# A hybrid attention layer in 4,804 matmuls: four edits to the order of weight splits, squares and loads

## The chip, the cores and the metric

The kernel runs on one core of a Trainium2 chip. The metric is the device time of one execution in microseconds (us); before the change it is 887.37 us, the median of three runs (884.22, 887.37, 887.9).

## What is computed

One decoder layer on 512 tokens of width 1024, in float32. Two token mixers run on the same normalised rows: gated linear attention (GLA, 4 heads, chunked) and multi-head latent attention (MLA, 8 heads, causal softmax). Each output is projected back, the two are merged by sigmoid gates, and projected once more. Then follows a squared-ReLU MLP of width 4096. Layer norms stand in front of the mixers and behind both sub-layers.

```python
h = layer_norm(x, ln_in_g, ln_in_b)
q_g, k_g, v_g, r_g, a_lr, q_lat, kv_lat, gate_logits = split(h @ w_in)
o_gla = rms_norm(gla_chunked(q_g * HK**-0.5, k_g, v_g, log_a), gla_norm_g)
y_gla = (o_gla * silu(r_g)) @ w_o_gla
q = rms_norm(q_lat, q_a_norm_g) @ w_q_b               # nope part, rope part
kv = rms_norm(kv_lat[..., :256], kv_a_norm_g) @ w_kv_b # k_nope, v
o_mla = causal_softmax_attention(q, k_nope, k_rope, v)  # blocks of 128 queries
y_mla = o_mla @ w_o_mla
mix = (g_gla * y_gla + g_mla * y_mla) @ w_out
h = layer_norm(ALPHA * h + mix, ln1_g, ln1_b)
h = layer_norm(ALPHA * h + square(relu(h @ w_ff1)) @ w_ff2, ln2_g, ln2_b)
```

## The kernel before

Every matmul keeps float32 precision with three products in a faster format: an operand is split into a rounded part `hi` and the rest `lo`, and the kernel adds hi x hi, hi x lo and lo x hi. So each weight tile passes through one fixed path. SP issues the load of a 512 KB raw tile (`wraw`, L175). ACT copies it to the rounded format (`whi` or `xh`, L190). DVE subtracts that from the raw tile (`wlo` or `xl`, L191). Then PE multiplies: L246 to L248 in `gemm_fm`, which puts features on the partitions, and L280 to L282 in `gemm_tm`, which puts tokens there.

All weight tiles stand in one list, `stream`, in the order in which the products use them. `pump(i)` is called as a product reaches tile i: it issues loads two tiles ahead and the splits one tile ahead (`DMA_AHEAD, SPLIT_AHEAD = 2, 1`). Tiles marked `res` are resident: they are split into buffers of their own. Everything else runs in generators that `tick` steps between the products of a weight tile. A scheduler then reorders the instructions of each engine, within the dependences and within the orders that `tc.issue_after` fixes; `issue_after` orders two instructions of the same engine and makes no engine wait for another. Entries of `st["gates"]` are such orders for the next split.

The places that the change touches, in order of time:

- The first layer norm. `ln_transpose` transposes each of eight 128-column blocks of the normalised rows on PE (L449), and evicts it: ACT writes the hi part `h` (L452) and, for some blocks, the temporary `lnt` (L454); DVE writes the other `lnt` (L456) and the lo part (L457). The products of the latent projections (`PL["lat", i]`, `gemm_tm`) take these blocks as they come. The two first tiles of q's weights follow in `stream`, and their splits are issued while these products run.
- GLA's output, `gla_out`, once for each of four heads. Four row blocks i of 128 tokens are computed (L891 to L893); blocks 0 and 1 share one PSUM tile, and so do 2 and 3. ACT squares each block with a sum (`osq`, L895); POOL raises the sums to the power -1/2, and DVE scales the blocks. Two lanes of generators share PE here: one for the heads' scores, one for these outputs.
- MLA. For each head and each block of queries PE computes the scores (L1006 to L1010), for block 0 with a reduce on DVE (L1003); DVE adds the mask and takes the maximum (`mx`, L1013), ACT the exponential (`Pm`, L1016), DVE the division (L1018). PE transposes the probabilities (L1030), and `split` writes them as `PT` (hi on ACT at L111, lo on DVE at L112). The products with v follow (L1049 to L1051). Beside the heads run the output products of GLA (`yg`) and MLA (`ym`), two halves of 512 columns each, with four weight tiles in a half. Scores, transposes and products with v share one ring of PSUM buffers, `px`.
- The middle layer norm (LN1) and the MLP's start. The first `w_ff1` products begin on half of the tokens, while the second half is still being normalised. Their first tiles are resident (`xh`, `xl`). At `ci == 0` of the loop over MLP slices, `win_load(0)` has POOL issue eight loads of `w_ff2`, 512 KB each (`wq`, L1425); `win_sums` on DVE (L1433) reads them later. POOL also computes the powers for the norm's rows (L433, two for each half of the tokens); DVE's L439 normalises the rows.

Of the kernel before, what the change touches and what calls it, by code (L numbers as in the profile page):

```python
# [10 lines left out]
F32 = mybir.dt.float32  # L11
# [4 lines left out]
AF = mybir.ActivationFunctionType  # L16
ALU = mybir.AluOpType
AX = mybir.AxisListType

P = 128  # L20
T = 512
# [6 lines left out]
HV = 256  # L28
# [24 lines left out]
def tile_hybrid_block(ctx: ExitStack, tc: tile.TileContext, I, out, dbg=None):  # L53
    nc = tc.nc
# [22 lines left out]
    def B(shape, dt=F32, n="b"):  # L77
        return pb.tile(shape, dt, tag="B", name=nm(n))

    def S(shape, dt=F32, n="s"):  # L80
        return sm.tile(shape, dt, tag=n, name=nm(n))
# [11 lines left out]
    def f(ap):  # L93
        return ap.bitcast(F32)

    act = nc.scalar.activation
    vtt = nc.vector.tensor_tensor
# [10 lines left out]

    def split(src, hi, lo, scale=None):
        if scale is None:  # L110
            act(hi, src, AF.Copy)  # L111
            return vtt(lo, src, f(hi), op=ALU.subtract)  # L112
        else:
            act(hi, src, AF.Copy, scale=scale)  # L114
            return stt(lo, src, scale, f(hi), op0=ALU.mult, op1=ALU.subtract)
# [22 lines left out]
    stream = []  # L138
    st = {"dma": 0, "spl": 0, "gates": ()}
# [38 lines left out]
    def pump(i):  # L178
        fetch(i + 1 + DMA_AHEAD)
        while st["spl"] < min(len(stream), i + 2 + SPLIT_AHEAD):  # L180
            e = stream[st["spl"]]
            if st["spl"] > i + e.get("ahead", SPLIT_AHEAD) and not e["res"]:
                break
            nk, n = e["nk"], e["n"]
            hi, lo = [A([P, nk, T * 2 // nk], F32R, w) for w in HOME["a" if e["res"] else e.get("home", "w")]]
            raw = e["src"]() if "src" in e else e.pop("raw")
            with ExitStack() as gates:
                for g in st["gates"]:
                    gates.enter_context(tc.issue_after(g.ins))
                st["ins"] = act(hi[:, :nk, :n], raw[:, :nk, :n], AF.Copy)  # L190
                st["lo"] = vtt(lo[:, :nk, :n], raw[:, :nk, :n], f(hi[:, :nk, :n]), op=ALU.subtract)  # L191
            st["gates"] = ()
            e["w"] = (hi, lo)
            if "post" in e:
                e["post"](raw)
            if "post2" in e:
                later[st["spl"] + 2] = lambda p=e["post2"], r=raw: p(r)
            later.pop(st["spl"], lambda: None)()
            st["spl"] += 1
# [11 lines left out]
    def spawn(g):  # L211
        active.append(g)
        return g
# [13 lines left out]
    def finish(*gs):  # L227
        while any(g in active for g in gs):
            for g in list(active):
                if g in gs:  # L230
                    step(g)
# [68 lines left out]
    half = LAT // 2  # L300
    PL = {}
# [92 lines left out]
    for mb in range(2):  # L394
        PL["ym", mb] = plan("w_o_mla", mb * T, T)

    def plan_zip(key, specs):
        pls = [{"idx": [], "nk": 8, "per": 2} for _ in specs]
        for k0 in range(0, 8, 2):
            for j, (name, c0, kb, res) in enumerate(specs):  # L400
                pls[j]["idx"] += plan(name, c0, T, kb + k0, kb + k0 + 2, res=res)["idx"]
        PL[key] = pls
# [39 lines left out]
    def ln_transpose(rows, g, b, outs, hf, alt=False, n="h0"):  # L442
        tk = slice(hf * 256, (hf + 1) * 256)
        for k in range(NK):
            if len(outs) <= k:
                outs.append(A([P, 2, T], F32R, n) if n == "h0" else (B([P, T], F32R, n), B([P, T], F32R, n)))
            p = MM() if alt and k in (4, 5) else PX()
            for i in range(2):
                nc.tensor.transpose(p[:, i * P:(i + 1) * P], rows[2 * hf + i][:, k * P:(k + 1) * P], ident)  # L449
            tmp = B([P, 256], F32, "lnt")  # L450
            hi, lo = part(outs[k], 0, tk), part(outs[k], 1, tk)
            ha = act(hi, p[:, :256], AF.Identity, scale=g[:, k:k + 1], bias=b[:, k:k + 1])  # L452
            if (alt or n == "h1") and k % 2:
                act(tmp, p[:, :256], AF.Identity, scale=g[:, k:k + 1], bias=b[:, k:k + 1])  # L454
            else:
                vts(tmp, p[:, :256], g[:, k:k + 1], b[:, k:k + 1], op0=ALU.mult, op1=ALU.add)  # L456
            hd = vtt(lo, tmp, f(hi), op=ALU.subtract)  # L457
            if n == "h1":
                st["ln"] = (ha, hd)
            yield hd  # L460

    mvin = consts.tile([P, NT, 2], F32, name="mvin")
# [73 lines left out]
    def ev_lat(i):  # L536
        def e(a, j, ps):
            if lat[a] is None:
                lat[a] = A([P, LAT], F32, "lat")
            if (a + i) % 2 == 0:  # L540
                nc.vector.tensor_copy(lat[a][:, i * half:(i + 1) * half], ps[:, :half])
            else:
                act(lat[a][:, i * half:(i + 1) * half], ps[:, :half], AF.Copy)
        return e
# [149 lines left out]
    def r_prep():  # L694
        for (fn, *args), wait in zip(((r_load, "t2"), (r_acc, "t2", "11"), (r_load, "t1"), (r_acc, "t2", "22"), (r_load, "t3"),
                                      (r_acc, "t1", "11"), (r_acc, "t3", "22")), RY):
            fn(*args)
            for _ in range(wait):
                yield
# [171 lines left out]
    def gla_out(h):  # L871
        while SS[h] is None or Vh[h] is None or rgn[h] < NT:
            yield
        sd, s128, s256 = SS[h]

        def blk(j, i, w):
            if i == j:
                return sd[:, w, i, :]
            if j // 2 == i // 2:
                return s128[:, w, j // 2, :]  # L880
            return s256[:, w, j, (i - 2) * P:(i - 1) * P]

        vh, vl = Vh[h]
        ss = S([P, NT], F32, "gss")
        ps = []
        for i in range(NT):
            if i % 2 == 0:
                ps.append(PX())
            o = ps[i // 2][:, (i % 2) * HV:(i % 2 + 1) * HV]
            for j in range(i + 1):  # L890
                mm(o, blk(j, i, 0), vh[:, j, :], start=j == 0, stop=False)  # L891
                mm(o, blk(j, i, 0), vl[:, j, :], start=False, stop=False)
                mm(o, blk(j, i, 1), vh[:, j, :], start=False, stop=j == i)  # L893
            sq = B([P, HV], F32, "osq")
            act(sq, o, AF.Square, accum_out=ss[:, i:i + 1])  # L895
            if i >= 1:
                yield
        vts(ss, ss, 4.0 / HV, 4.0 * RMS_EPS, op0=ALU.mult, op1=ALU.add)
        rs = S([P, NT], F32, "grs")
        gtt(rs, ss, mhalf[:, :NT], op=ALU.pow)  # L900
        yield
        og = [B([P, 2, HV], F32, "og") for _ in range(2)]
        for i in range(NT):
            o = ps[i // 2][:, (i % 2) * HV:(i % 2 + 1) * HV]
            stt(og[i // 2][:, i % 2, :], o, rs[:, i:i + 1], Rg[h][:, i, :], op0=ALU.mult, op1=ALU.mult)
        yield
        for kk in range(2):
            k = 2 * h + kk
            p = PX()
            for tt in range(NT):  # L910
                nc.tensor.transpose(p[:, tt * P:(tt + 1) * P], og[tt // 2][:, tt % 2, kk * P:(kk + 1) * P], ident)
            yield
            o = A([P, 2, T], F32R, "ogT")
            split(p, o[:, 0, :], o[:, 1, :], scale=glg[:, k:k + 1])
            ogT[k] = o
# [70 lines left out]
    def mla_head(h, hl, qn, kn, vt):  # L986
# [39 lines left out]
        for b, (pl, pt) in enumerate(zip(plan_t, PT)):  # L1026
            n = len(pl) * P
            p = PX()
            for cc, j, i in pl:
                nc.tensor.transpose(p[:, cc * P:(cc + 1) * P], Ps[i][:, j * P:(j + 1) * P], ident)  # L1030
            split(p[:, :n], pt[:, 0, :], pt[:, 1, :])
            if b != 1:
                yield
        PT0, PT1, PT2 = PT
# [68 lines left out]
    for hf in range(2):  # L1103
        if hf == 1:
            finish(t_ln1)
            t_prep = spawn(prep())
            t_rp = spawn(r_prep())
        for i in range(2):
            gemm_tm([PL["lat", i]], hT, half, ev_lat(i), tts=(2 * hf, 2 * hf + 1))
    t_lat = spawn(latents())  # L1110
    t_he = spawn(h_early())
    gemm_fm(PL["q"], hT, T, ev_q)
# [306 lines left out]
    def win_load(ci):  # L1419
        w2 = I["w_ff2"].rearrange("(k p) n -> p k n", p=P)  # L1420
        for op, i, j in (("12", 0, 1), ("11", 0, 0), ("22", 1, 1), ("21", 1, 0)):
            for hf in range(2):
                t = A([P, 2, T], F32, "wq")
                k0 = 8 * ci + 4 * hf + i
                nc.gpsimd.dma_start(t, w2[:, k0:k0 + 3:2, j * T:(j + 1) * T])  # L1425
                WQ[("f2", ci), (op, hf)] = t
# [106 lines left out]
    for ci in range(FC):  # L1533
# [1 line left out]
        hid = []  # L1535
        win = ci < FC - 1
        if ci == 0:
            win_load(0)

        def ev_h(a, ps):  # L1540
            r = B([P, T], F32, "relu")
# [127 lines left out]
```

## Time and profile before

| | before |
|---|---|
| median of 3 runs | 887.37 us (884.22 to 887.9) |
| profiled execution | 886.19 us, of which the span is 884.3 us |
| PE busy | 863.6 us (98% of the span) |
| DVE, ACT, POOL busy | 639.8, 469.5, 197.7 us |
| mean granted clock of PE | 0.996 |
| bytes moved | 134.60 MB, 152 GB/s on average |

PE is TensorE, PEld its weight loads, DVE VectorE, ACT ScalarE, POOL GpSimd and SP SyncE. A timeline row gives the start in us from the span's start, the duration, the engine, the source line, the operation, what it writes and reads with shapes, how often, and in brackets the engine's idle time before it with what ended it. PEclk is the share of the full clock that the throttle granted to PE. A row with "x4" stands for four like instructions, and its duration is that of all four.

### The profile page before, as it was taken

How to read it: one execution, taken by the hardware profiler on the slowest of the kernel's cores; microseconds unless marked ns; L12 is line 12 of the kernel's file. 1: busy time of each engine (PE TensorE's matmuls, PEld its weight loads, DVE VectorE, ACT ScalarE, POOL GpSimd, SP SyncE). 2: the span in 40 equal slices, each digit the busy share in tenths (PEclk: the TensorE clock that was granted, in tenths of full speed). 3: DMA queues.
4: the chain of work that ended last, by engine and by line, in shares of the span. 5: the costliest groups of instructions: out<-in, count | busy, mean ns of one | idle time of the engine just before them, and what ended most of it. 6: DMA issues, size and time to landing. Idle time of an engine off the chain costs nothing.

```text
span 884.3 us, 13010 instructions
## 1 busy us (share of the span) xinstructions
PE 863.6 (98%) x4804; PEld 754.6 (85%) x4804; DVE 639.8 (72%) x1042; ACT 469.5 (53%) x823; POOL 197.7 (22%) x225
## 2 busy tenths in 40 slices
PE   6999999999999999999999999999999999999996
PEld 5988888889999978888888888988888888889985
DVE  7849969968665646757776796987557646788865
ACT  5546756646475634435554414566357546656820
POOL 1223637944201030300000013004400520141001
PEclk9999999999999999999999999999999999999999
DMA  7994936694738454322216527006941990399312
GB/s 242 281 228 136 321 117 151 221 247 147 216 71 223 126 148 103 102 66 72 78 41 249 187 83 275 1 1 168 292 111 30 263 252 28 83 233 232 119 62 82
DMA packets 95504, 134.60 MB, mean 152 GB/s; under 512 B 12960, under 2 KB 58400, under 8 KB 95440
## 3 DMA queue, kind: packets, MB, share of 16 engines
q1 hardware_dynamic: 73840, 92.36, 33.1%
q0 software_dynamic: 19392, 37.76, 19.9%
q10 hardware_dynamic: 2208, 3.66, 1.2%
q8 instruction: 38, 0.62, 0.3%
q14 instruction: 26, 0.21, 0.1%
HBM read 110.15 MB, written 8.91 MB: 135 GB/s over the span
## 4 chain that ended last, share of the span: by engine, by line
PE 93%; DVE 3%; DMA 2%; ACT 1%; issue 1%; POOL 0%; POOLq 0%; SPq 0%; DVEq 0%; ACTq 0%
PE mm L246 11%; PE mm L247 11%; PE mm L248 11%; PE mm L280 4%; PE mm L282 4%; PE mm L281 4%; PE mm L1194 4%; PE mm L1196 4%; PE mm L1195 4%; PE px L1482 2%; PE px L1481 2%; PE px L1480 2%; PE px L848 2%; PE mm L1482 2%; PE mm L1481 2%; PE mm L1480 2%
## 5 line engine op out<-in xcount | busy, mean ns | idle before, releaser
L191 DVE TENSOR_TENSOR wlo<-wraw,whi 128x1024 fp32r<-128x1024 f32 (+1 forms) x90 | 100.4, 1116 | 87.0 <-ACT whi L190 83.5
L190 ACT ACTIVATE whi<-wraw 128x1024 fp32r<-128x1024 f32 (+1 forms) x90 | 85.4, 949 | 86.4 <-PE mm L247 43.4
L246 PE MATMUL mm<-h,whi 128*128 128x512 f32 x224 | 87.3, 390 | 0.0
L247 PE MATMUL mm<-h,whi 128*128 128x512 f32 x224 | 87.2, 389 | 0.0
L248 PE MATMUL mm<-h,wlo 128*128 128x512 f32 x224 | 83.0, 390 | 0.0
L1499 POOL DMA_DIRECT2D res<-ev x42 | 36.8, 994 | 178.9 <-ACT ev L1497 143.4
L191 DVE TENSOR_TENSOR wlo<-wq,whi 128x1024 fp32r<-128x1024 f32 x44 | 54.5, 1239 | 30.1 <-ACT whi L190 30.1
L190 ACT ACTIVATE whi<-wq 128x1024 fp32r<-128x1024 f32 x44 | 46.5, 1057 | 26.1 <-PE mm L1195 16.1
L1195 PE MATMUL mm<-sh,whi 128*128 128x256 f32 x176 | 49.9, 283 | 0.0
L1196 PE MATMUL mm<-sh,wlo 128*128 128x256 f32 x176 | 49.9, 283 | 0.0
L1194 PE MATMUL mm<-sh,whi 128*128 128x256 f32 x176 | 49.9, 283 | 0.0
L248 PEld LDWEIGHTS mm<-h,wlo 128*128 128x128 f32 x224 | 42.0, 188 | 9.0 <-DVE wlo L191 0.4
L247 PEld LDWEIGHTS mm<-h,whi 128*128 128x128 f32 x224 | 42.1, 188 | 8.7
L246 PEld LDWEIGHTS mm<-h,whi 128*128 128x128 f32 x224 | 42.1, 188 | 8.7
L190 ACT ACTIVATE xh<-wraw 128x1024 fp32r<-128x1024 f32 (+1 forms) x28 | 27.3, 984 | 28.8 <-PE mm L282 14.5
L433 POOL TENSOR_TENSOR mv<-mv,mhalf 128x1 f32<-128x1 f32 x4 | 4.1, 1031 | 164.7 <-DVE mv L432 164.7
L191 DVE TENSOR_TENSOR xl<-wraw,xh 128x1024 fp32r<-128x1024 f32 (+1 forms) x28 | 31.3, 1129 | 10.6 <-ACT xh L190 10.6
L792 ACT ACTIVATE E<-rp 128x256 f32<-128x256 f32 x64 | 26.0, 418 | 22.5 <-POOL rp L787 15.6
L1542 ACT ACTIVATE relu<-mm 128x512 f32<-128x512 f32 x24 | 14.1, 596 | 41.5 <-PE mm L248 41.5
L786 POOL TENSOR_TENSOR rp<-rp 128x256 f32<-128x256 f32 x32 | 30.0, 937 | 25.4 <-ACT E L792 16.7
L787 POOL TENSOR_TENSOR rp<-rp 128x256 f32<-128x256 f32 x32 | 33.7, 1053 | 7.4 <-ACT q L817 3.8
L962 POOL DMA_DIRECT2D QS<-q x32 | 16.1, 509 | 85.3 <-ACT q L114 82.1
(477 smaller groups left out, 2816.6 us busy)
## 6 DMA issues: line engine op xcount, KB each, us to landing
wraw<-in_w_ff_dram SPq DMA_DIRECT2D x36, 512.0 KB, 5.0
wraw<-in_w_in_dram SPq DMA_DIRECT2D x30, 512.0 KB, 4.8
wq<-in_w_ff_dram POOLq DMA_DIRECT2D x26, 512.0 KB, 9.8
res<-ev POOLq DMA_DIRECT2D x42, 256.0 KB, 10.1
wq<-in_w_in_dram SPq DMA_DIRECT2D x20, 512.0 KB, 6.7
wq<-in_w_in_dram POOLq DMA_DIRECT2D x18, 512.0 KB, 10.5
hsd<-hs SPq DMA_DIRECT2D x16, 256.0 KB, 4.9
xr<-hsd SPq DMA_DIRECT2D x16, 256.0 KB, 4.1
```

The costliest lines, as they stand in the source:

```text
L190: st["ins"] = act(hi[:, :nk, :n], raw[:, :nk, :n], AF.Copy)
L191: st["lo"] = vtt(lo[:, :nk, :n], raw[:, :nk, :n], f(hi[:, :nk, :n]), op=ALU.subtract)
L246: mm(o, hi[:, c], xh, start=first, stop=False)
L247: mm(o, hi[:, c], xl, start=False, stop=False)
L248: mm(o, lo[:, c], xh, start=False, stop=last)
L280: mm(o, xh, hi[:, :n], start=opens, stop=False, skip_group_check=share)
L281: mm(o, xh, lo[:, :n], start=False, stop=False, skip_group_check=share)
L282: mm(o, xl, hi[:, :n], start=False, stop=last, skip_group_check=share)
L1194: mm(oa, hi[:, k, c], xh, start=opens and k == 0 and a == 0, stop=False, skip_group_check=True)
L1195: mm(oa, hi[:, k, c], xl, start=False, stop=False, skip_group_check=True)
L1196: mm(oa, lo[:, k, c], xh, start=False, stop=k == 3, skip_group_check=True)
L1499: nc.gpsimd.dma_start(res[tt + t][:, j * T:(j + 1) * T], e, accum_op=ALU.add)
```

## The change

Four edits; all computed values stay the same.

1. `ln_transpose` keeps the two instructions that evict block 5 of the first half of the tokens. `lat_guard`, called at the end of the products of the second latent tile, puts the next split (the second q tile's) behind those two, each in its engine's order.
2. In `gla_out` the square of block 0 is issued behind the products of block 1, together with block 1's own square, in each head. The sums and the number of instructions stay as they are.
3. The weight tiles of `yg` half 1 and of both halves of `ym` are split one 512-column half at a time, hi then lo (12 instructions more on ACT, 12 more on DVE). The second tile of `ym` half 0 is split behind the last pair of instructions that wrote transposed probabilities, `st["pt"]`.
4. At `ci == 0` POOL copies one column of the lo part of the third `w_ff1` tile to a 128x1 tile, `tok`, and the first loads of `w_ff2` are placed behind that copy in POOL's order. The copy needs DVE's subtraction of that tile, so here POOL does wait for another engine.

Order and number of all other instructions: PE has the same 4,804 matmuls. On PE, ACT and DVE the order of the two builds differs up to the end of the LN1 stretch and is the same from there on. SP's order differs by one exchange of two neighbouring loads.

```diff
@@ -108,7 +108,7 @@
 
     def split(src, hi, lo, scale=None):
         if scale is None:
-            act(hi, src, AF.Copy)
+            st["hi"] = act(hi, src, AF.Copy)
             return vtt(lo, src, f(hi), op=ALU.subtract)
         else:
             act(hi, src, AF.Copy, scale=scale)
@@ -185,10 +185,11 @@
             hi, lo = [A([P, nk, T * 2 // nk], F32R, w) for w in HOME["a" if e["res"] else e.get("home", "w")]]
             raw = e["src"]() if "src" in e else e.pop("raw")
             with ExitStack() as gates:
-                for g in st["gates"]:
+                for g in st["gates"] or (st.get("pt", ()) if e.get("late") else ()):
                     gates.enter_context(tc.issue_after(g.ins))
-                st["ins"] = act(hi[:, :nk, :n], raw[:, :nk, :n], AF.Copy)
-                st["lo"] = vtt(lo[:, :nk, :n], raw[:, :nk, :n], f(hi[:, :nk, :n]), op=ALU.subtract)
+                for k in [slice(i, i + 1) for i in range(nk)] if e.get("fine") else [slice(0, nk)]:
+                    st["ins"] = act(hi[:, k, :n], raw[:, k, :n], AF.Copy)
+                    st["lo"] = vtt(lo[:, k, :n], raw[:, k, :n], f(hi[:, k, :n]), op=ALU.subtract)
             st["gates"] = ()
             e["w"] = (hi, lo)
             if "post" in e:
@@ -394,6 +395,11 @@
     for mb in range(2):
         PL["ym", mb] = plan("w_o_mla", mb * T, T)
 
+    for key in (("yg", 1), ("ym", 0), ("ym", 1)):
+        for i in PL[key]["idx"]:
+            stream[i]["fine"] = True
+    stream[PL["ym", 0]["idx"][1]]["late"] = True
+
     def plan_zip(key, specs):
         pls = [{"idx": [], "nk": 8, "per": 2} for _ in specs]
         for k0 in range(0, 8, 2):
@@ -457,6 +463,8 @@
             hd = vtt(lo, tmp, f(hi), op=ALU.subtract)
             if n == "h1":
                 st["ln"] = (ha, hd)
+            elif hf and k == 5:
+                st["h0"] = (ha, hd)
             yield hd
 
     mvin = consts.tile([P, NT, 2], F32, name="mvin")
@@ -891,8 +899,9 @@
                 mm(o, blk(j, i, 0), vh[:, j, :], start=j == 0, stop=False)
                 mm(o, blk(j, i, 0), vl[:, j, :], start=False, stop=False)
                 mm(o, blk(j, i, 1), vh[:, j, :], start=False, stop=j == i)
-            sq = B([P, HV], F32, "osq")
-            act(sq, o, AF.Square, accum_out=ss[:, i:i + 1])
+            for r in ((), (0, 1), (2,), (3,))[i]:
+                sq = B([P, HV], F32, "osq")
+                act(sq, ps[i // 2][:, r % 2 * HV:(r % 2 + 1) * HV], AF.Square, accum_out=ss[:, r:r + 1])
             if i >= 1:
                 yield
         vts(ss, ss, 4.0 / HV, 4.0 * RMS_EPS, op0=ALU.mult, op1=ALU.add)
@@ -1028,7 +1037,8 @@
             p = PX()
             for cc, j, i in pl:
                 nc.tensor.transpose(p[:, cc * P:(cc + 1) * P], Ps[i][:, j * P:(j + 1) * P], ident)
-            split(p[:, :n], pt[:, 0, :], pt[:, 1, :])
+            lo = split(p[:, :n], pt[:, 0, :], pt[:, 1, :])
+            st["pt"] = (st["hi"], lo)
             if b != 1:
                 yield
         PT0, PT1, PT2 = PT
@@ -1105,8 +1115,12 @@
             finish(t_ln1)
             t_prep = spawn(prep())
             t_rp = spawn(r_prep())
+
+        def lat_guard():
+            finish(t_ln1)
+            st["gates"] = st["h0"]
         for i in range(2):
-            gemm_tm([PL["lat", i]], hT, half, ev_lat(i), tts=(2 * hf, 2 * hf + 1))
+            gemm_tm([PL["lat", i]], hT, half, ev_lat(i), tts=(2 * hf, 2 * hf + 1), guard=lat_guard if i and not hf else None)
     t_lat = spawn(latents())
     t_he = spawn(h_early())
     gemm_fm(PL["q"], hT, T, ev_q)
@@ -1535,7 +1549,10 @@
         hid = []
         win = ci < FC - 1
         if ci == 0:
-            win_load(0)
+            lo = stream[PL["f1", 0, 0]["idx"][2]]["w"][1]
+            tok = nc.gpsimd.tensor_copy(S([P, 1], F32, "tok"), f(lo[:, 1, T - 1:T]))
+            with tc.issue_after(tok.ins):
+                win_load(0)
 
         def ev_h(a, ps):
             r = B([P, T], F32, "relu")
```

## Prediction, made before the changed kernel was run

> **What bounds the kernel now.** I read the page first (busy shares and the chain that ended last), then the list of PE's waits, then windows around the longest of them with their granted clock, then the timeline at each place that the diff touches.
>
> ```profile
> span 884.3 us, 13010 instructions
> PE 863.6 (98%) x4804; PEld 754.6 (85%) x4804; DVE 639.8 (72%) x1042; ACT 469.5 (53%) x823; POOL 197.7 (22%) x225
> PE 93%; DVE 3%; DMA 2%; ACT 1%; issue 1%; POOL 0%; POOLq 0%; SPq 0%; DVEq 0%; ACTq 0%
> ```
>
> PE is busy for 863.6 of 884.3 us and is 93% of the chain. No PE instruction is added, removed or resized by the diff, so all that it can move is what PE does not work: 20.7 us, and time at a lower clock. PE's waits (columns: line, what was waited for, total us, times, longest):
>
> ```profile
> engine line waited for: us in total, times, longest us
> PE px L449 <- DMA wraw<-in_w_in_dram: 8.7, 1, 8.7
> PE px L1049 <- DVE mx L1013: 1.6, 1, 1.6
> PE px L449 <- ACT lnt L454: 1.5, 1, 1.5
> PE px L891 <- ACT osq L895: 0.5, 1, 0.5
> PE mm L280 <- ACT h L452: 0.5, 1, 0.5
> PE px L449 <- DVE lnt L456: 0.3, 1, 0.3
> ```
>
> The 8.7 us is the first load, which the diff leaves alone. The other five rows, 4.4 us together, lie each at a place that the diff edits. That is the most that removed waits can bring, apart from the clock:
>
> ```profile
> core 0: us, PE busy (x) PEld busy (x) DVE busy (x) ACT busy (x) POOL busy (x), PEclk, DMA share, GB/s
> 430.60:434.00 3.40, 1.76 (x8) 1.14 (x8) 2.66 (x5) 3.40 (x8) 0.00 (x0) 1.00 0.16 43
> 434.00:437.40 3.40, 3.40 (x10) 2.79 (x9) 2.11 (x6) 0.12 (x2) 0.00 (x0) 0.51 0.36 137
> ...
> 536.40:539.80 3.40, 1.93 (x10) 1.24 (x8) 0.92 (x1) 2.01 (x4) 1.21 (x2) 1.00 1.04 396
> 539.80:543.20 3.40, 3.28 (x17) 2.46 (x18) 3.33 (x10) 3.40 (x8) 0.00 (x0) 1.00 1.03 374
> ```
>
> In 430.6 to 434.0 PE works 1.76 of 3.40 us, and the next 3.40 us run at a clock of 0.51: 3.40 x (1 - 0.51) = 1.67 us of work lost behind a wait of 1.6 us. In 536.4 to 539.8 PE works 1.93 of 3.40 us, nearly as little, and no lower clock follows. So an idle stretch of this length sometimes draws a half-clock stretch of 1.67 us and sometimes doesn't. The three timed runs (884.22, 887.37 and 887.9) and the profiled one (886.19) lie in steps of such a size.
>
> The profiled execution took 886.19 us, 1.9 more than its span, and lies 1.2 us under the median of 887.37. The sum below is made against 886.19.
>
> **First part: the second q tile's split is held (27 to 32 us).** ACT's 29.19 row is the hi half of that split, DVE's 30.28 row its lo half:
>
> ```profile
> 29.19 1.06 ACT L190 ACTIVATE whi<-wraw 128x1024 fp32r<-128x1024 f32 x1 [0.56 <-DMA wraw<-in_w_in_dram]
> ```
>
> ```profile
> 30.28 1.23 DVE L191 TENSOR_TENSOR wlo<-wraw,whi 128x1024 fp32r<-128x1024 f32 x1 [0.39 <-ACT whi L190]
> ```
>
> They stand in ACT's and DVE's order ahead of the evictions of ln_transpose (h, lnt), for which PE waits 0.5 and 0.3 us. The change puts them behind the sixth of the eight evictions: h is up to 1.06 us earlier, the lo half of h up to 1.23 us. Both waits are shorter than that and go: **-0.8 us**. Queued behind the held split is the next weight load on SP, which needs its raw buffer, and the loads of r behind it in SP's queue. The products with q's weights start only here:
>
> ```profile
> 48.71 0.39 PE L246 MATMUL mm<-h,whi 128*128 128x512 f32 x1
> ```
>
> That is 17 us behind the split as it stood (48.71 less 30.28 and 1.23), more than a hold to the sixth eviction can take, so both the split and the load are hidden; if that cover were gone, PE would wait at most the slip itself. Bounds: 0 (the wait moves to the seventh eviction) to -0.87, the whole 0.8 with the rounding of two rows.
>
> **Second part: the first square of a GLA head goes behind the second product.** L895 squares block i = 0 in the PSUM tile which the products of i = 1 (L891) then write:
>
> ```profile
> 251.18 0.39 ACT L895 ACTIVATE osq<-px 128x256 f32<-128x256 f32 x1 [2.12 <-PE px L893]
> ...
> 252.21 0.39 PE L891 MATMUL px<-vh,s 128*128 128x256 f32 x1 [0.54 <-ACT osq L895]
> ```
>
> With both squares behind the products of i = 1 that wait is gone: -0.54. Only one of four heads shows it; in the others PE had other products to put in. Against it: the tile is held for one more square, 0.39 us, before the norm can be formed, in four heads, and the scheduler reorders much of what lies between 150 and 260 us. Bounds: -0.54 to +1.6 (four more waits of 0.39). I take **-0.5**, from the only row that shows such a wait.
>
> **Third part: the output products' splits by halves, and ym0's second behind the transposed probabilities (430 us).** Before, a full-tile split stood ahead of a score block (L1013) and the probabilities' split (L111, L112):
>
> ```profile
> 430.24 1.06 ACT L190 ACTIVATE whi<-wraw 128x1024 fp32r<-128x1024 f32 x1 [0.24 <-ACT Pm L1016]
> 431.21 1.07 ACT L111 ACTIVATE PT<-px 128x512 fp32r<-128x512 f32 x2
> ...
> 431.34 1.23 DVE L191 TENSOR_TENSOR wlo<-wraw,whi 128x1024 fp32r<-128x1024 f32 x1 [0.74 <-ACT whi L190]
> 432.48 0.55 DVE L1013 CUSTOM_DVE_ANT_0 P<-px,masks 128x384 f32<-128x384 f32 x1
> 432.95 1.28 DVE L112 TENSOR_TENSOR PT<-px,PT 128x512 fp32r<-128x512 f32 x2
> ...
> 433.19 0.47 PE L1049 MATMUL px<-PT,mv 128*128 128x512 f32 x1 [1.61 <-DVE mx L1013]
> ```
>
> PE's L1049 waits for a PSUM buffer that L1013 reads, L1013 stands behind the lo half, and that behind the hi half. Without the two, ACT's first PT half can start from 430.24, where the split stood; I take 430.4 to 431.0 (half of 1.07, rounded up for the transposes ahead of it), DVE's first from 431.05 to 431.7 (half of 1.28), and L1049 starts at about 431.9 in place of 433.19: -1.3 us. What is late next: the second ym0 tile can no longer fill PE while the next head's scores wait for DVE's reduce. That opens a wait of its own near 439 us:
>
> ```profile
> 445.44 0.41 DVE L1003 TENSOR_REDUCE P<-px 128x128 f32<-128x256 f32 x1
> ```
>
> One such reduce with the eviction in front of it is 0.41 plus about 0.3 us: +0.7. The half-clock stretch hung on a wait of 1.6 us; the two left are 0.35 and 0.7, so I let it go: -1.67. The halves add 12 instructions each to ACT and DVE (three outputs, four tiles each). A half costs 0.54 on ACT and 0.64 on DVE by the PT rows, against 0.53 and 0.62 for half a tile: under 0.15 us more for each tile, on engines busy 53% and 72%, hidden by the weight tile in hand; uncovered, it would be 12 x 0.04 = 0.4 us. Sum: -1.3 + 0.7 - 1.67 = **-2.3 us**. Bounds: -3.3 (wait and stretch gone, no new one) to +1 (the first wait stays for half a split and the new one costs a full split, with the stretch kept).
>
> [...]
>
> **Fourth part: w_ff2's loads wait for the third w_ff1 tile (524 to 540 us).** POOL issues the eight w_ff2 loads (L1425), ACT's split at 537.79 is late for want of its tile, and the LN1 evictions stand behind it, for which PE waits 1.5 us:
>
> ```profile
> 524.02 2.24 POOL L433 TENSOR_TENSOR mv<-mv,mhalf 128x1 f32<-128x1 f32 x2 [151.82 <-DVE mv L432]
> 529.62 2.93 POOL L1425 DMA_DIRECT2D wq<-in_w_ff_dram  x4 [3.36 <-issue]
> ```
>
> On DVE, the split that the added copy waits for, and the reader of the w_ff2 tiles:
>
> ```profile
> 527.02 2.36 DVE L191 TENSOR_TENSOR xl<-wraw,xh 128x1024 fp32r<-128x1024 f32 x2
> ...
> 550.73 1.23 DVE L1433 TENSOR_TENSOR T<-wq,wq 128x1024 f32<-128x1024 f32 x1
> ```
>
> On ACT, the late split:
>
> ```profile
> 537.79 1.06 ACT L190 ACTIVATE whi<-wraw 128x1024 fp32r<-128x1024 f32 x1 [4.12 <-DMA wraw<-in_w_ff_dram]
> ```
>
> The queues from 533.0 to 537.8 us (q0 carries w_ff2, q1 w_ff1; packets, MB, share of the DMA engines):
>
> ```profile
> q0 software_dynamic: 413, 1.53, 89.0%
> q1 hardware_dynamic: 95, 0.09, 6.4%
> ```
>
> The same from 531 to 532, when only q1 moves anything:
>
> ```profile
> q1 hardware_dynamic: 338, 0.33, 105.5%
> ```
>
> In 4.8 us the w_ff1 tile gets only its last 0.09 MB through, beside 1.53 MB of w_ff2; alone it moved 0.33 MB in one us, so it lacked about 0.3 us of an empty queue. The tile for whose lo half the added copy (128x1, on POOL) waits is the second of the 527.02 row: done at 529.38. The copy costs about half of the 2.24 us for two L433, or less, so the first load is issued at 530.0 to 530.6 rather than 529.62. A delay of 0.4 to 1.0 us against 0.3 missing: it should let the tile land by about 533.5, some 4 us earlier, and PE's idle time in the two windows goes, 3.40 - 1.93 + 3.40 - 3.28 = 1.59: **-1.6 us**. Queued behind the copy on POOL are the eight loads, and behind them the second pair of L433. The loads are 512 KB each, 4.2 MB, which at 1.53 MB in 4.8 us takes 13 us, from 533 to about 546; their reader, DVE's L1433, starts at 550.73, so a slip of 1 us stays inside some 4 us of cover. If that were gone, L1433 would hold up LN1's L439 behind it by as much as the loads are late. Bounds: -1.6 to +1 (the loads' slip passed on whole).
>
> Sum: 886.19 - 0.8 - 0.5 - 2.3 - 1.6 = 881.0 us. Against the median it is 6.4 less (0.72%), against the profiled run 5.2.
>
> **The rivals.** [...]
>
> *The fourth part does nothing.* The first four loads are issued over 2.93 us anyway, so holding the first by 0.4 us moves the bulk of their bytes little, and the tile still trickles beside w_ff2. For it: the margin is 0.1 to 0.7 us. Against: 0.33 MB in one us is more than three times what is missing. 881.0 + 1.6 = 882.6; with the first rival, 884.3.
>
> *The GLA stretch gets slower.* The deferred square holds the PSUM tile longer, and PE waits for it in all four heads. It decides when the hold (0.39 and the queue on ACT) outgrows PE's other products there, and a wait reaches the 1.6 us at which the clock fell at 431. Then 4 x (1.6 + 1.67) = 13.1, and 881.0 + 0.5 + 13.1 = 894.6. Against it: ACT's 53%, and PE waiting there once only, for 0.54. With waits alone, of 0.39 each, it would be 881.0 + 0.5 + 1.6 = 883.1.
>
> **How the numbers follow.** Forecast 0.52; clock rival 0.17; fourth part without effect 0.14; both 0.06; slower through the GLA stretch, or through w_ff2's late loads, 0.08; short new waits of some 3 to 5 us that eat the gain, 0.03. 0.5% of 887.37, about what a measurement of this kernel can tell from no change, is 4.4 us: faster ends at 882.9. The forecast lies under it, and so do somewhat over two in five of the two single rivals, as the runs scatter by some 2 us: 0.52 + 0.13 = 0.65 faster. Same: 0.18 of these + 0.06 + 0.03 = 0.27. Slower 0.08. The range: downwards the lower bounds of the four (-0.87, -0.54, -3.3, -1.6: 879.9) and three quarters of the 2.0 us by which the run of 884.22 lies under that of 886.19: 878.4. Upwards both rivals at once, 884.3, and the 1.2 us from the profiled run to the median: 885.5.
>
> **What would show it.** Of the profile after: no wait of L449 at 27 to 32 us; no wait of L891 for osq; L1049 waiting under 0.6 us near 432, with a new wait under 1 us near 439 and no window under a clock of 0.9 from 420 to 450; ACT's split landing near 533.5 rather than 537.79, and no wait of L449 for lnt at 539. From 560 us on, PE's order is as before, so the lead has to stand by then and stay level to the end. I am wrong if PE's busy time changes by more than the lost clock, if w_ff2's first sums run later than 553 us, or if new PE waits in 150 to 260 us add up to over 1 us.

## The result, and the profile after

The changed kernel takes 881.43 us (median of 6 runs, 880.45 to 882.47) against 886.41 us for the kernel before (6 runs, the three named at the start among them, 883.88 to 889.37): a ratio of 0.9944, interval 0.992 to 0.9968. Run again with 12 executions beside 23 of the kernel before, it gave 882.48 against 886.68 us, 0.996 (0.9944 to 0.9975). It is faster by 0.4 to 0.6%.

The profiled execution took 882.47 us. PE's waits in it (same view as before; the changed file is longer, so L455 is the former L449, L1059 the former L1049, and L191 and L192 the former L190 and L191):

```profile
engine line waited for: us in total, times, longest us
PE px L455 <- DMA wraw<-in_w_in_dram: 8.4, 1, 8.4
PE px L1210 <- DVE wlo L192: 2.0, 1, 2.0
PE px L1015 <- DVE P L1012: 0.5, 1, 0.5
PE px L1495 <- DVE wlo L192: 0.5, 1, 0.5
PE mm L247 <- ACT h L458: 0.3, 1, 0.3
PE mm L1210 <- DVE wlo L192: 0.3, 1, 0.3
PE mm L247 <- DVE rt L960: 0.2, 1, 0.2
PE px L1059 <- DVE PT L112: 0.2, 1, 0.2
PE px L455 <- DVE lnt L462: 0.2, 1, 0.2
```

The waits for mx (1.6), for lnt in LN1 (1.5), for osq (0.5) and for h in the first layer norm (0.5) are gone. L1059 waits 0.2 where L1049 waited 1.6, and the reduce of the next head (L1012) costs 0.5. New, and foreseen at no place, are 2.8 us in three waits for DVE's splits, all between 780 and 796 us, where all orders are those of the kernel before. The clock around the place of the former wait for mx (L1049 started at 433.19, L1059 starts at 428.98):

```profile
core 0: us, PE busy (x) PEld busy (x) DVE busy (x) ACT busy (x) POOL busy (x), PEclk, DMA share, GB/s
427.00:430.40 3.40, 3.19 (x20) 2.74 (x20) 2.81 (x8) 2.82 (x8) 0.00 (x0) 1.00 0.21 81
430.40:433.80 3.40, 3.40 (x22) 2.89 (x20) 2.62 (x9) 1.16 (x4) 0.00 (x0) 1.00 0.00 0
433.80:437.20 3.40, 2.88 (x19) 2.37 (x19) 1.59 (x4) 1.92 (x5) 0.00 (x0) 1.00 0.00 0
```

PE idles 0.21 and 0.52 us in these windows, and the clock stays at 1.00. So far this looks like the prediction at work. The question for the experiments is whether the waits that went had stood in every execution of the kernel before.

### The profile page after: what moved, and what is told of

Read it like the earlier page. It is cut to its first block, busy times and chain, and to the rows that moved or that the text cites. A ratio compares the mean times of both kernels' runs of the same rounds, so it can differ in the third digit from the quotient of the medians.

```text
span 880.7 us, 13019 instructions
## 1 busy us (share of the span) xinstructions
PE 861.2 (98%) x4804; PEld 752.9 (85%) x4804; DVE 643.2 (73%) x1054; ACT 470.2 (53%) x835; POOL 198.3 (23%) x226
## 4 chain that ended last, share of the span: by engine, by line
PE 92%; DVE 3%; DMA 2%; ACT 1%; issue 0%; POOLq 0%; SPq 0%; DVEq 0%; POOL 0%; ACTq 0%
PE mm L247 11%; PE mm L248 11%; PE mm L249 11%; PE mm L283 5%; PE mm L281 5%; PE mm L282 5%; PE mm L1210 4%; PE mm L1209 4%; PE mm L1208 4%; PE px L856 2%; PE px L1495 2%; PE px L1494 2%; PE px L1496 2%; DMA res<-ev 2%; PE mm L755 2%; PE mm L754 2%
## 5 line engine op out<-in xcount | busy, mean ns | idle before, releaser
L192 DVE TENSOR_TENSOR wlo<-wraw,whi 128x1024 fp32r<-128x1024 f32 (+1 forms) x102 | 102.0, 1009 | 82.3 <-ACT whi L191 79.2
L191 ACT ACTIVATE whi<-wraw 128x1024 fp32r<-128x1024 f32 (+1 forms) x102 | 86.5, 860 | 86.0 <-PE mm L248 46.6
L192 DVE TENSOR_TENSOR wlo<-wq,whi 128x1024 fp32r<-128x1024 f32 x44 | 54.5, 1238 | 28.0 <-ACT whi L191 27.9
L191 ACT ACTIVATE whi<-wq 128x1024 fp32r<-128x1024 f32 x44 | 46.5, 1056 | 28.4 <-PE mm L1209 20.0
L191 ACT ACTIVATE xh<-wraw 128x1024 fp32r<-128x1024 f32 (+1 forms) x28 | 27.2, 985 | 28.6 <-PE mm L283 16.7
L192 DVE TENSOR_TENSOR xl<-wraw,xh 128x1024 fp32r<-128x1024 f32 (+1 forms) x28 | 31.3, 1128 | 8.5 <-ACT xh L191 8.5
```

The costliest lines, as they stand in the source:

```text
L191: st["ins"] = act(hi[:, k, :n], raw[:, k, :n], AF.Copy)
L192: st["lo"] = vtt(lo[:, k, :n], raw[:, k, :n], f(hi[:, k, :n]), op=ALU.subtract)
```

## The experiments

**The kernel before, a second profile.** No edit.

> The kernel before once more, for a second profile. If the half-clock stretch of 3.4 us at 434 follows from the wait of 1.6 us in front of it, it comes again at the same place. [...]

It took 881.61 us, 4.6 less than its first profile, and PE waited for this (beside 8.3 us for the first load):

```profile
PE px L1049 <- DVE mx L1013: 1.6, 1, 1.6
PE px L891 <- ACT osq L895: 0.5, 1, 0.5
PE px L449 <- DVE lnt L456: 0.3, 1, 0.3
PE mm L246 <- ACT h L452: 0.3, 1, 0.3
PE mm L246 <- DVE rt L951: 0.2, 1, 0.2
```

The wait of 1.6 us for mx is there, the half-clock stretch behind it is not, LN1's wait for lnt (L454) is not, and the first layer norm's wait of L280 for h isn't either (the row with h that is left is another, near 553 us). So three of the rows on which the prediction's sum stood are not in every execution. Over all profiles of this document, LN1's wait for lnt stands in one, the wait of L280 for h in five of the eight without the first edit (0.4 to 0.9 us), and in the seven profiles of kernels that keep the mx wait of 1.6 us (the two of before among them) the clock fell behind it once: the mean granted clock is 0.996 in that profile, 0.997 to 0.999 in the other six.

**The fourth edit alone, and the change without it.**

The first adds these lines to before, the second takes them out of the changed kernel:

```diff
+            lo = stream[PL["f1", 0, 0]["idx"][2]]["w"][1]
+            tok = nc.gpsimd.tensor_copy(S([P, 1], F32, "tok"), f(lo[:, 1, T - 1:T]))
+            with tc.issue_after(tok.ins):
                 win_load(0)
```

> Before plus the fourth edit alone (POOL's copy of a column of the third w_ff1 tile ahead of the first w_ff2 loads). PE's, DVE's and SP's orders are those of before. Theory 'copy' (as predicted): the first w_ff2 load is issued 0.4 to 1.0 us later against PE's work, the w_ff1 tile lands some 4 us earlier, PE's wait of 1.5 us for ACT's lnt near 539 goes, and the run is about 1.6 us shorter than before's profiled run. Rival 'order': the first load waits anyway for its buffer, which PE releases, longer than for the copy; so the copy changes nothing, the wait of about 1.5 us stays, and the time is before's.

> The changed kernel without the fourth edit. PE's, DVE's and SP's orders are those of the changed kernel. 'Copy': PE's wait of about 1.5 us for lnt near 532 comes back, and the time is some 1.6 us above the changed kernel's (about 883). 'Order': no such wait, since the first three edits moved a split of a w_ff1 tile between the two row normalisations of LN1 and so freed the raw buffers for the next loads 1 to 2 us earlier; the time is the changed kernel's (about 881.4).

The copy alone took 882.43 us in one execution, against 881.61 for the undisturbed one of before, and PE's waits had no lnt in LN1; since before's second profile hadn't either, time and waits settle nothing there. For the changed kernel the other run does: without the copy 881.6 us in 12 runs (ratio 0.9948, 0.9925 to 0.997), with it 882.48 in 12 on the same chip, so the copy gains nothing. POOL's rows, first of the changed kernel, then of the one without the copy:

```profile
522.59 0.18 POOL L1553 COPY tok<-xl 128x1 f32<-128x1 f32 x1 [4.16 <-DVE xl L192]
524.84 2.93 POOL L1439 DMA_DIRECT2D wq<-in_w_ff_dram  x4 [2.07 <-issue]
```

```profile
524.82 2.92 POOL L1439 DMA_DIRECT2D wq<-in_w_ff_dram  x4 [6.06 <-issue]
```

With the copy POOL is free at 522.77 and still issues its first load at 524.84; without it, at 524.82. The time called "issue" is a wait of POOL's sequencer: by the program's semaphores, for PE's last product with the tile whose buffer the load takes over. That product (L283) starts at 523.85, takes 0.40 us and so ends at 524.25, later than the copy, so the gate holds nothing back. In the changed kernel the expectation "order" held.

In before's order it does not quite hold, for there the copy comes last. With the copy alone:

```profile
527.57 0.18 POOL L1539 COPY tok<-xl 128x1 f32<-128x1 f32 x1 [3.18 <-DVE xl L191]
528.13 2.21 POOL L1425 DMA_DIRECT2D wq<-in_w_ff_dram  x3 [0.38 <-issue]
```

The first load goes out 0.2 us later than without the copy (15.72 against 15.49 in the table below), 0.60 us behind SP's third w_ff1 load, and it is 0.60 us again in the change without the third edit, the other profile with the copy in that order. In the four profiles of before's order without it, that distance is 0.22 to 1.19 us. So there the copy sets a least distance, as the prediction meant it to; in the changed kernel it has nothing to set.

What goes with a late split is how long before w_ff2's first load SP has issued the last of the three w_ff1 loads that fall there. From the timelines of eight profiles (lead: the second column less the first), in us from the start of the first w_ff1 product:

```
kernel                     third w_ff1 load  first w_ff2 load  second late split  PE waits for lnt
before, first profile           15.27             15.49             23.65              1.5
copy alone                      15.11             15.72             21.47              none
before, second profile          14.45             15.49             19.22              none
first edit alone                14.29             15.49             19.25              none
halves alone                    15.02             15.94             20.13              none
change without copy             14.01             15.95             20.05              none
change, second profile          13.84             15.95             18.86              none
change, first profile           13.66             15.95             19.11              none
```

With 0.2 us between the two loads the split comes at 23.65 (one profile), with 0.6 us at 21.47 (PE can just stand that), and from 0.9 us on at 18.9 to 20.1. In the changed kernel the lead is 1.9 to 2.3 us, and the third edit brought that, not the copy: DVE now splits a w_ff1 tile between the two row normalisations instead of ahead of both. That order alone doesn't make the whole lead, since each half of the third edit has it too, with 0.9 us (halves alone) and 1.5 us (order alone, below).

**The copy taken from a later tile**, so that it really holds the loads.

```diff
-            lo = stream[PL["f1", 0, 0]["idx"][2]]["w"][1]
-            tok = nc.gpsimd.tensor_copy(S([P, 1], F32, "tok"), f(lo[:, 1, T - 1:T]))
+            lo = stream[st["spl"] - 1]["w"][1]
+            tok = nc.gpsimd.tensor_copy(S([P, 1], F32, "tok"), f(lo[:, 3, 255:256]))
```

> Before plus the fourth edit with its copy taken from the next split (the first w_ff1 tile of the later slices), so that the first w_ff2 load really waits: issued at about 19.9 us behind the start of the w_ff1 products rather than 15.5. PE's and DVE's orders are those of before. 'Late loads block' (the slower side of the prediction): w_ff2 lands some 4 us later, DVE's first sums L1433 with it, L439 stands behind them and PE waits in LN1's second half, more than the 0.5 us that stands there in every profile, by up to 4 us. 'Covered': the w_ff1 tiles land early (the second split starts before 20 us), the first sums start when they did, and PE's waits between 524 and 560 us are those of the undisturbed profile of before (0.5 and 0.2).

```profile
532.46 0.18 POOL L1539 COPY tok<-wlo 128x1 f32<-128x1 f32 x1 [8.24 <-DVE wlo L191]
533.02 5.81 POOL L1425 DMA_DIRECT2D wq<-in_w_ff_dram  x8 [0.38 <-issue]
...
546.04 1.23 DVE L1433 TENSOR_TENSOR T<-wq,wq 128x1024 f32<-128x1024 f32 x1
```

The loads start 5.1 us later (20.60 us behind the first w_ff1 product, against 15.49), the late split starts at 19.85, DVE's first sum in its usual place (33.6 us, as in before's second profile), and PE's waits in LN1 are 0.3 and 0.2 as ever (882.37 us). "Covered" held: the prediction's 4 us of cover were a low guess.

**The third edit alone, and the change without it.** The first is before with only the `st["hi"]`, `fine`, `late` and `st["pt"]` lines of the diff, the second the changed kernel without them:

```diff
+    for key in (("yg", 1), ("ym", 0), ("ym", 1)):
+        for i in PL[key]["idx"]:
+            stream[i]["fine"] = True
+    stream[PL["ym", 0]["idx"][1]]["late"] = True
```

> Before plus the third edit alone (splits of yg and ym by halves, ym0's second tile behind the transposed probabilities). Its order in LN1 is that of the changed kernel: one w_ff1 split stands between the two row normalisations. Theory 'third edit carries it': PE's wait at 431 falls from 1.8 us to 0.4, a new one of 0.7 us stands some 8 us later, and the third SP load of w_ff1 is issued 13.6 to 14.0 us behind the start of the w_ff1 products rather than 14.5 to 15.3, so that its tile lands by 20 and LN1's wait for lnt (1.6 us in one of three profiles of the old order) is missing; the waits of the first edit (0.3 to 1.4 us near 30) and of the second (0.5 near 251) stay. Time about 883. Rival 'each edit its own': LN1's wait is as in the old order, now and then 1.6 us. On the late waits (781 to 795): 'chance' has them missing or present without rule; 'order' has over 0.8 us here.

> The changed kernel without the third edit (first, second and fourth stay). 'Third edit carries it': PE waits 1.8 us at 431, LN1's order is the old one, with the third SP load of w_ff1 issued at 14.5 to 15.3 us and a wait for lnt now and then; the waits of the first and second edits are gone (0.8 to 1.9 us together). Time about 885. Rival 'each edit its own': the copy keeps LN1's wait away and the time is about 883.5. Late waits at 781 to 795: 'order' none, 'chance' without rule.

The third edit alone: 883.43 us in 10 runs (ratio 0.9969, 0.9951 to 0.9987). Without it: 884.14 in 10 runs (0.9971, 0.9951 to 0.999). The two parts of the change are worth 0.3% each. In the profiles PE's idle time at 415 to 450 us is 2.2 us with the third edit and 3.0 without, and LN1 shows no lnt wait in either, so that the two theories aren't told apart there by the wait, only by the loads' lead (2.2 us with the third edit, 0.6 without).

**Halves alone, order alone.** Before with the third edit's code, but in the one without the last of the lines above, in the other without the three ahead of it:

```diff
-    stream[PL["ym", 0]["idx"][1]]["late"] = True
```

```diff
-    for key in (("yg", 1), ("ym", 0), ("ym", 1)):
-        for i in PL[key]["idx"]:
-            stream[i]["fine"] = True
```

> Before plus the splits by halves alone, without the order behind the transposed probabilities. If the halves carry the gain at 431, the wait of 1.8 us there falls to 1.2 or less, since the score block stands behind half a split (0.6 rather than 1.2 us). If the order carries it, 1.8 us or a little less stay, and the wait of 0.7 us some 8 us later is missing. LN1's order of splits has one split between the two normalisations, so no wait for lnt near 539.

> Before plus the order of ym0's second split behind the transposed probabilities alone, with whole-tile splits. If the order carries the gain at 431, the wait there falls from 1.8 us to about 0.4, and a wait of 0.7 to 1.3 us stands near 439 (the second tile is split late, as a whole). If the halves are needed, 1.2 us or more stay in the two together beyond the changed kernel's 1.1.

PE's wait at 431 us, first with halves alone, then two rows with the order alone:

```profile
PE px L1055 <- DVE mx L1018: 1.2, 1, 1.2
```

```profile
PE px L1009 <- DVE P L1006: 0.5, 1, 0.5
...
PE px L1053 <- DVE PT L112: 0.2, 1, 0.2
```

The order does the work: 1.6 falls to 0.2, and the reduce's 0.5 appears. Halves alone leave 1.2. Idle time at 415 to 450 us is 3.2 before, 2.8 with halves, 2.5 with the order, 2.2 with both. (Single executions: 881.58 with halves, 885.18 with the order; 3.9 us of the latter are the late waits below.)

**The first edit alone, the second alone.** Before with the lines of the diff for the one or the other:

```diff
+        def lat_guard():
+            finish(t_ln1)
+            st["gates"] = st["h0"]
```

```diff
+            for r in ((), (0, 1), (2,), (3,))[i]:
+                sq = B([P, HV], F32, "osq")
+                act(sq, ps[i // 2][:, r % 2 * HV:(r % 2 + 1) * HV], AF.Square, accum_out=ss[:, r:r + 1])
```

> Before plus the first edit alone. As predicted: no wait of L280 for h and none of L449 for lnt between 27 and 33 us (0.3 to 1.4 us in three profiles of the old order), 0.8 to 1.4 us gained there and no new wait before 60 us. Rival: the wait moves to a later eviction, and the idle time of PE between 27 and 40 us stays above 0.5 us. All else as in the old order: 1.8 us at 431, 0.5 at 251; no late waits if 'order' holds for them.

> Before plus the second edit alone. As predicted: L891's wait for osq (0.5 us, 0.7 of idle issue, in each of three profiles of the old order) is gone and nothing takes its place between 150 and 260 us: -0.5 to -0.7. Rival: the later square holds the PSUM tile, and new waits of some 0.39 us in each of four heads take it back, up to +1. Else as in the old order: 1.8 us at 431, waits near 30 us; no late waits if 'order' holds for them.

Both did as predicted where they act. The idle time of PE beyond the usual distance of its matmuls, summed over the gaps of each stretch (us, from the traces):

```
                          24-40   240-262   415-450   515-565   775-812
before, first profile      2.1      1.1       4.8       3.6       0.0
before, second profile     1.6      1.1       3.2       1.5       0.0
copy alone                 2.5      1.2       3.2       1.5       0.0
copy of a later tile       2.0      1.1       3.2       1.5       0.0
first edit alone           0.4      1.1       3.2       1.4       4.1
second edit alone          1.9      0.2       3.2       1.4       0.0
halves alone               1.6      1.1       2.8       1.5       0.0
order alone                1.7      1.1       2.5       1.5       3.9
third edit alone           2.2      1.2       2.2       1.5       1.1
change without third       1.0      0.2       3.0       1.5       0.0
change without copy        0.4      0.1       2.2       1.5       1.0
change, second profile     0.4      0.1       2.2       1.5       1.2
change, first profile      0.5      0.1       2.2       1.5       3.6
```

Each of the first three edits takes its share in its own stretch wherever it is; the last column is another matter, taken up next. (120 to 240 us is 5 to 6 us in all of them, so the reordered GLA stretch cost nothing that these sums show.) The first edit's single execution took 885.75 us for the late waits' sake, the second's 881.16.

**The changed kernel, a second profile.** No edit.

> The changed kernel once more, on the same chip as the run without the fourth edit. In its first profile (882.47 us) PE waited 3.2 us near 781 to 795 us for DVE splits, which before's profile doesn't have; other executions took 880.5. If these waits are a matter of chance in the DMA traffic there, a second profile shows them larger, smaller or not at all, and its time moves with them (880.5 without, 882 and more with them). If they follow from PE being some 7 us earlier there, they come again with 2 to 3 us.

Something of each: the waits came again, but with 1.2 us of idle time instead of 3.6, and this execution took 879.75 us. They go back to ACT, whose eviction `ev` waits for the DMA that adds an earlier `ev` to the rows, and so frees its buffer; the next splits stand behind it. The row in three kernels: change, first profile; change, second; before, second:

```profile
773.28 0.60 ACT L1511 ACTIVATE ev<-mm 128x512 f32<-128x512 f32 x1 [4.83 <-DMA res<-ev]
```

```profile
770.57 0.60 ACT L1511 ACTIVATE ev<-mm 128x512 f32<-128x512 f32 x1 [2.66 <-DMA res<-ev]
```

```profile
772.02 0.60 ACT L1497 ACTIVATE ev<-mm 128x512 f32<-128x512 f32 x1 [0.66 <-DMA res<-ev]
```

An ACT wait of 4.83 us goes with 3.6 us of idle PE, 2.66 with 1.2, 0.66 with none. The third edit's order is not their only cause: the first edit alone, which has none of it, had 4.1 us. But it isn't cleared either. All five profiles of kernels with the order behind the transposed probabilities have late waits, and of the eight without it (halves alone among them) only the first edit alone has. By what way it would act some 350 us later, no run shows.

**More room for these evictions**, in the changed kernel:

```diff
-                    if ci < FC - 2 or n < 10:
+                    if ci < FC - 2 or n < 5:
```

> The changed kernel with one number changed: in the last but one MLP slice the evictions of ACT go to larger tiles with their own buffers from phase 5 on (`n < 5` in place of `n < 10`), so that two of them (and one more later) no longer wait for an accumulating DMA to free their buffer. PE's order is the changed kernel's. Theory: the late waits at 781 to 795 us (1.0 to 3.6 us in every profile with the third edit's order) come from ACT's eviction that waits for such a DMA, with the splits behind it in ACT's queue. Then they are gone, the stretch from the middle of LN1 to the end takes 327.6 us as in most profiles of the old order (328.6 to 331.2 with the waits), and the time is about 880 (881.4 to 882.5 for the changed kernel). Rival: the loads of that stretch are late of themselves; the waits stay at 1 us or more and only move to the split's own load.

It was meant to be faster than both kernels, and it is slower than both: 891.93 us in 6 runs, ratio to before 1.0063 (1.0039 to 1.0086). The three views are PE's wait, ACT's wait, and three windows with the clock (columns as above).

```profile
PE px L1208 <- ACT whi L191: 10.1, 1, 10.1
```

```profile
ACT T L1511 <- DMA res<-T: 14.3, 1, 14.3
```

```profile
793.80:797.20 3.40, 0.00 (x0) 0.00 (x0) 0.00 (x0) 0.00 (x0) 0.55 (x1) 0.74 1.15 239
797.20:800.60 3.40, 0.00 (x0) 0.00 (x0) 0.00 (x0) 0.62 (x2) 0.00 (x0) 0.50 1.13 234
...
804.00:807.40 3.40, 3.40 (x25) 3.40 (x24) 1.63 (x2) 1.01 (x2) 0.00 (x0) 0.76 1.10 276
```

PE's waits at 781 and 790 us are gone, and of the longest one, at 795 us, 0.5 is left, as the theory has it. But the larger tile holds two evictions, its next user waits for both additions, and these were issued late on POOL: ACT stood 14.3 us, PE 10.1, and the clock went to one half, from 795.4 to 805.6 us as worked out from the means of 0.74 and 0.76. So the place is most likely right (ACT behind an adding DMA), and the remedy was wrong.

## Why the prediction was right or wrong

The time was right: 881.0 forecast, 881.43 measured, inside the range. By the prediction's own border of 0.5% the first series (0.56%) is "faster", to which it gave 0.65, and the second (0.40%) would be "same", with 0.27. The hit is in part luck: 3.3 of the 5.2 us forecast were two terms (-1.67 and -1.6) that before's second execution didn't contain at all. The four steps of the sum:

1. *First part, forecast -0.8.* Right in kind, too small: 1.6 to 2.5 us of idle issue time without the edit, 0.4 to 1.0 with it, so about -1.4. The mis-sized step is the bound of 0.87: it was made of the two waits of the view, 0.5 and 0.3, where the gaps between the matmuls of the same profile sum to 2.1. Of those two waits the one for lnt (0.3) was in all eight profiles without the edit, the one for h in five.
2. *Second part, forecast -0.5.* Right: -1.0, of which 0.5 is the wait itself. The slower rival (GLA waits in all four heads) found nothing: 120 to 240 us is unchanged.
3. *Third part, forecast -2.3, made of -1.3, +0.7 and -1.67.* The first two were right: 1.6 of wait became 0.2, the foreseen new one 0.5; idle time from 3.2 to 2.2, so -1.0 where -0.6 was said. The -1.67 was wrong as a step: the half-clock stretch "hung on a wait of 1.6 us" in the prediction, and it stood in one of seven profiles with that wait; in the other six the wait came without it. That the stretch would come again at one of the shorter waits left, on which the clock rival's 0.17 and the 884.3 in the range rest, no run shows: in both profiles of the change the clock reads 1.00 there (427.0 to 437.2 us, and 424 to 444).
4. *Fourth part, forecast -1.6.* Wrong. In the changed kernel the copy doesn't delay w_ff2's first load (524.84 with it, 524.82 without), and the wait it was to remove isn't in every execution. The failed step is the one from 529.62 to "530.0 to 530.6": it left DVE's split where it stood before. The third edit moves that split ahead, so the copy is done at 522.77, and what is left of the 3.36 us called "issue" is POOL's wait for a buffer that PE frees. In before's order the step holds, with 0.60 us between the loads and no wait for lnt in both profiles. So the rival in which the fourth part does nothing had the outcome right, but not the reason. The sign that the prediction named came true all the same: the split starts 19.1 us behind the first w_ff1 product, where "533.5" would be 19.4. The third edit's lead of about 2 us did that.

Of the 5.2 us forecast, 1.9 were of the kind that lasts (-0.8 - 0.5 - 0.6), and they turned out at about 3: PE starts the 1700th matmul from the end, in the middle of LN1, at 542.4 and 542.1 us in the two profiles of the change, at 545.1 in before's second. From there to the last matmul it is 327.6 us in before's two profiles and 331.2 and 328.8 in the change's, so 1 to 4 us are given back by the late waits. The prediction had said that the lead would stay level from 560 us on; that sign failed. It gave short new waits a chance of 0.03. Another of its signs, PE's busy time changing by more than the lost clock (863.6 to 861.2 us, against 1.67), was drawn too tight: before's second profile is as low, at 861.4.

Why then do the medians lie 4 to 5 us apart, and not 2? Most likely because before's median contains such events, as its first profile did. Its 23 runs go from 882.14 to 894.01, and their mean granted clock stands for 3.2 us lost on average (span times one less the clock, run by run), against 2.7 us in the 12 runs of the change: 0.5 us of the difference. With that taken off, the means are 883.2 and 879.5. An undisturbed run of before would be 881.6 less some 1.8 us lost to the clock, 879.9; so its runs lose another 3.3 us on average to waits like LN1's, the first layer norm's and the late ones. How often each comes wasn't seen: timed runs carry no profile. The profiles see too few of them, it seems: where a profiled execution is one of several runs, it was the shortest in four series of six, and before's second profile (881.61) lies under all 23 runs. That the change makes LN1's wait rarer is made likely by the loads' lead; that this explains the rest of the gap is only argued. Left open too is why the adding DMAs that ACT waits for land early in seven of these thirteen profiles and late in six: the order of instructions is the same there in all of them, and two profiles of the very same kernel differ by 2.4 us. All five profiles with the third edit's order are among the late, and the order alone had 3.9 us, in its one profile. That points at this order or at something that differs with it; no run separates the two.

## What to carry to other kernels

A wait in one profile is a wait of one execution. Before costing its removal, profile the same kernel again: here the waits for mx and osq came in every profile that kept their order, and the edits against them gave what they promised or more; LN1's wait and the clock stretch came once. And before adding a wait to hold a transfer back, look at what its queue is already waiting for, in the order of the changed kernel: idle time in front of a DMA issue (2.07 us here) may be a wait for a buffer's release that no view names.

## What the runs showed of the hardware

The clock fell after a wait of 1.6 us in one of seven profiles, with PE at work for 1.76 of the 3.40 us before it, and read 0.51 on the mean of the 3.40 us that followed (before, first profile, 434.0 to 437.4). In the other six profiles with that wait PE's idle time at 415 to 450 us is 3.0 to 3.2 us against 4.8, and in two of them (before, second profile; copy alone) the clock reads 1.00 in every window from 424 to 444 us. A longer wait did not bring it down: in the first profile of the change PE waits 2.0 us for a split until 795.34, and the windows around it read

```profile
793.40:796.80 3.40, 1.46 (x12) 1.46 (x13) 3.37 (x6) 2.58 (x4) 2.09 (x3) 1.00 1.07 318
796.80:800.20 3.40, 3.40 (x31) 3.40 (x30) 2.46 (x3) 2.01 (x3) 0.00 (x0) 1.00 1.08 287
```

So in these runs neither the length of the wait (1.6 us with a fall once, 2.0 without) nor PE's work in 3.40 us (1.76 with, 1.46 without) tells by itself whether the clock falls.

In the kernel with the 10.1 us wait it fell about 4 us into the wait (1.00 up to 793.8, 0.74 on the mean of 793.8 to 797.2, then 0.50) and came back about 4 us after work resumed (0.50 up to 804.0, 0.76 on the mean of 804.0 to 807.4, then 1.00).

A product of 256 columns took 378 ns in float32 (L856) and 283 ns in the rounded format (L1194), both in the first profile of before.

Two loads on different queues whose issues lay 0.2 us apart went with a split of the earlier one's tile 4.4 us later than a lead of 1.0 us did (23.65 and 19.22 us, two profiles of one kernel): its last 0.09 MB went through beside 1.53 MB of the other.
